# The mask of the soft-max: a GpSimd add one slot ahead in place of a bf16 matmul

## The chip, the core and the metric

The kernel runs on one core of a Trainium2 chip. The metric is device time in microseconds (us) of one execution. Five engines work side by side, each through its own queue in order: TensorE (PE: matmuls and transposes into PSUM), VectorE (DVE), ScalarE (ACT), GpSimd (POOL), and SyncE (SP), which issues the DMAs.

## The reference

Two layers over 512 positions of width 1024. Each projects `x`, runs two groups of eight attention heads, gates them, projects back and normalises. Group A is stick-breaking attention. Group B, to which the change belongs, is soft-max attention over the keys that an indexer picks:

```python
score = jnp.where(admissible[None], score, -jnp.inf)
vals, idx = lax.top_k(score, topk)
...
logits = jnp.einsum('bqhd,bqkhd->bqhk', qb, kg).astype(jnp.float32) * scale
bias = rel_bias[t5_bucket(idx - t[None, :, None])]
logits = logits + jnp.swapaxes(bias, -1, -2).astype(jnp.float32)
logits = jnp.where(valid[:, :, None, :], logits, -jnp.inf)
p = jax.nn.softmax(logits, axis=-1)
```

The kernel gathers nothing: it computes all logits of a block of 128 queries against the keys up to that block and adds a mask that is 0 for picked keys and -1e30 for the others.

## The kernel before, in words

Work is cut into blocks: one head, 128 queries (`qb` 0 to 3), with n = 128, 256, 384 or 512 keys. A layer has 24 blocks of the indexer, 32 of group A (`Stick`), 32 of group B (`Soft`); each starts in a slot of its own, slots 0 to 87 of the loop over `s`. The Soft blocks are slots 56 to 87: eight heads of four blocks, so `qb` is the slot's number modulo 4. The order of instructions on PE, ACT, DVE and POOL is the order of the code.

A Soft block passes through four slots:

- slot s: `stage0` puts the logits `z` into PSUM (a matmul at L399, the mask's at L401, a matmul at L402; the operands are split into a high and a low part). `z` has two PSUM buffers. `stage1` (DVE, L599) adds the position bias `gbias`, negates, writes `p` and keeps the row's minimum; `stage1b` (ACT, L604) takes the exponential and its row sums.
- slot s+1: `stage2`. In the last pair of heads (slots 80 to 87) it scales `p` by the reciprocal of the sums (L613 on DVE, L614 on ACT). In the other heads the reciprocals go through DRAM (`spread`), come back as the tile `over`, and POOL multiplies the pair's output by it later (L550).
- slot s+2: PE transposes `p` (L407), ACT copies the result to `AT` (L415), and DVE writes what that copy rounded off (L418).
- slot s+3, where the head's fourth block is that far: PE multiplies by the values (`o`, L556), ACT and DVE bring the two halves of `o` together (`mixt`, L464 and L466), and POOL multiplies them into `M` (L467). That is in slots 58, 62, ..., 86 for the head before.

Around these steps a slot is filled with projection matmuls (`pj`, `pjv`, `pjo`), by a table of due slots. Their weights come by DMA (`raw`), ACT rounds them to `whi` (L175), and POOL forms `wlo`, two instructions of 512 columns (L177). In slots 76, 79, 81 and 85 (`SPLITS`) ACT and POOL also split `M` for the output projection: `XH` on ACT (L144), then `XL` on POOL (L145).

On DVE, slot s has L599 of block s ahead of L418 of block s-2, and both ahead of `mixt`. On ACT, the exponential of block s stands ahead of the `XH` of that slot and of the copy of `mixt`.

## Time and profile before

| | |
|---|---|
| median of 3 runs | 674.58 us (674.5 to 675.34) |
| profiled execution, its own time | 674.73 us |
| its span, first to last instruction | 672.9 us |
| busy: PE, DVE, ACT, POOL | 659.6, 482.7, 351.5, 330.6 us |
| granted TensorE clock, mean | 0.997 |

The span is what the trace shows; the execution's time is 1.8 us longer. Busy shares are means over the whole span; what an engine's time is worth is read stage by stage. In the trace the Soft slots run from 208 to 298 us in the first layer and from 538 to 628 us in the second.

### The profile page before, as it was taken

The numbers are of one execution on the slowest core, as the hardware profiler recorded it, in microseconds if no ns is written. First come the engines' busy times: TensorE is split into PE (matmuls) and PEld (weight loads), VectorE is DVE, ScalarE is ACT, GpSimd is POOL, SyncE is SP. The second block draws the span as 40 slices with busy tenths as digits, with TensorE's granted clock in tenths as the row PEclk, the third lists the DMA queues.
The fourth block names the chain that finished last, engine by engine and source line by source line (L and its number), as shares of the span: only waits on it lengthen the run. The fifth ranks groups of instructions, "written<-read, shape, count | busy, mean of one in ns | idle before, by whom it ended". The sixth has DMA issues, their size and how long they took to land.

```text
span 672.9 us, 10299 instructions
## 1 busy us (share of the span) xinstructions
PE 659.6 (98%) x3575; PEld 553.7 (82%) x3589; DVE 482.7 (72%) x1019; ACT 351.5 (52%) x707; POOL 330.6 (49%) x303
## 2 busy tenths in 40 slices
PE   8999999999999999999999999999999999999995
PEld 4778988988889879877897888889888898897784
DVE  3588899999855455666853689999989554556576
ACT  4576545445447556773233765544534565568610
POOL 5343634466564433764354344445566533457531
PEclk9999999999999999999999999999999999999998
DMA  7625224242342354212125143432114534442022
GB/s 247 221 82 146 95 94 126 64 128 92 99 140 82 115 142 152 82 52 94 41 82 171 64 120 101 126 94 94 64 63 142 126 111 123 123 148 68 32 94 94
DMA packets 26203, 72.85 MB, mean 108 GB/s; under 512 B 5124, under 2 KB 6788, under 8 KB 26152
## 3 DMA queue, kind: packets, MB, share of 16 engines
q1 hardware_dynamic: 26152, 72.20, 34.4%
q8 instruction: 28, 0.46, 0.3%
q14 instruction: 23, 0.19, 0.1%
HBM read 58.87 MB, written 2.31 MB: 91 GB/s over the span
## 4 chain that ended last, share of the span: by engine, by line
PE 88%; DVE 5%; POOL 2%; DMA 2%; issue 1%; ACT 1%; SPq 1%; DVEq 0%; POOLq 0%; ACTq 0%
PE pj L221 14%; PE pj L222 14%; PE pj L223 14%; PE o L556 6%; PE tr L407 5%; PE z L402 4%; PE pjo L642 4%; PE pjo L644 4%; PE pjo L641 4%; PE z L399 4%; PE pjv L249 4%; PE pjv L248 4%; PE pjv L247 4%; POOL wlo L177 1%; DMA XN<-in_xt_dram 1%
## 5 line engine op out<-in xcount | busy, mean ns | idle before, releaser
L177 POOL TENSOR_TENSOR wlo<-raw,whi 128x512 fp32r<-128x512 f32 (+1 forms) x168 | 228.0, 1378 | 157.7 <-ACT whi L175 139.7
L221 PE MATMUL pj<-XH,whi 128*128 128x512 f32 (+1 forms) x456 | 185.4, 407 | 0.4 <-ACT whi L144 0.4
L222 PE MATMUL pj<-XL,whi 128*128 128x512 f32 (+1 forms) x456 | 178.9, 392 | 0.8 <-DVE XL L145 0.8
L223 PE MATMUL pj<-XH,wlo 128*128 128x512 f32 (+1 forms) x456 | 179.2, 393 | 0.0
L223 PEld LDWEIGHTS pj<-XH,wlo 128*128 128x128 f32 (+1 forms) x456 | 84.9, 186 | 20.3 <-POOL wlo L145 0.4
L175 ACT ACTIVATE whi<-raw 128x1024 fp32r<-128x1024 f32 (+1 forms) x87 | 91.2, 1050 | 19.9 <-PE pjo L642 6.6
L222 PEld LDWEIGHTS pj<-XL,whi 128*128 128x128 f32 (+1 forms) x456 | 85.4, 187 | 15.3 <-DVE XL L145 2.4
L221 PEld LDWEIGHTS pj<-XH,whi 128*128 128x128 f32 (+1 forms) x456 | 85.3, 187 | 15.1 <-ACT whi L144 1.1
L247 PE MATMUL pjv<-whi,XH 128*128 128x256 f32 x256 | 75.3, 294 | 0.0
L569 ACT ACTIVATE om<-z 128x128 f32<-128x128 f32 (+1 forms) x64 | 27.9, 437 | 86.9 <-PE z L402 80.7
L575 DVE TENSOR_TENSOR_SCAN om<-om 128x128 f32<-128x128 f32 (+1 forms) x64 | 69.3, 1082 | 5.1 <-POOL om L571 4.9
L249 PE MATMUL pjv<-wlo,XH 128*128 128x256 f32 x256 | 72.5, 283 | 0.3 <-POOL wlo L177 0.3
L248 PE MATMUL pjv<-whi,XL 128*128 128x256 f32 x256 | 72.2, 282 | 0.0
L467 POOL TENSOR_TENSOR M<-M,mixt 64x512 f32<-64x512 f32 x22 | 32.0, 1452 | 72.7 <-DVE mixt L466 39.3
L688 DVE MAX8 m<-scores 128x8 f32<-128x256 f32 (+2 forms) x96 | 52.8, 550 | 0.2
L689 DVE MATCH_REPLACE8 scores<-m,scores 128x256 f32<-128x256 f32 (+2 forms) x96 | 52.1, 542 | 0.0
L641 PE MATMUL pjo<-whi,XH 128*128 128x512 f32 x128 | 51.7, 404 | 0.0
L642 PE MATMUL pjo<-whi,XL 128*128 128x512 f32 x128 | 50.1, 391 | 1.6 <-DVE XL L145 1.6
L418 DVE TENSOR_TENSOR AT<-tr,AT 128x128 fp32r<-128x128 f32 (+1 forms) x64 | 31.3, 490 | 27.9 <-ACT AT L415 27.6
L644 PE MATMUL pjo<-wlo,XH 128*128 128x512 f32 x128 | 50.0, 391 | 0.0
L402 PE MATMUL z<-k,q 128*128 128x256 f32 (+2 forms) x128 | 49.3, 385 | 0.0
L249 PEld LDWEIGHTS pjv<-wlo,XH 128*128 128x128 f32 x256 | 48.6, 190 | 0.7 <-POOL wlo L177 0.7
(125 smaller groups left out, 1192.3 us busy)
## 6 DMA issues: line engine op xcount, KB each, us to landing
raw<-in_w_in_dram SPq DMA_DIRECT2D x70, 512.0 KB, 3.3
k<-k SPq DMA_DIRECT2D x32, 256.0 KB, 5.2
raw<-in_w_out_dram SPq DMA_DIRECT2D x16, 512.0 KB, 3.4
gbias<-f_dram SPq DMA_DIRECT2D x16, 256.0 KB
XN<-in_x_dram SPq DMA_DIRECT2D x4, 512.0 KB
out_dram<-XN SPq DMA_DIRECT2D x8, 256.0 KB, 2.1
M<-M SPq DMA_DIRECT2D x4, 448.0 KB
XN<-in_xt_dram SPq DMA_DIRECT2D x3, 512.0 KB
```

The source lines that it names most:

```text
L175: A.activation(hi[:, :n], raw[:, :n], AF.Copy)
L177: lo_engine.tensor_tensor(lo[:, c], raw[:, c], hi[:, c], ALU.subtract)
L221: T.matmul(o, w[0], XH[:, :, kc, :], start=first, stop=False)
L222: T.matmul(o, w[0], XL[:, :, kc, :], start=False, stop=False)
L223: T.matmul(o, w[1], XH[:, :, kc, :], start=False, stop=last)
L247: T.matmul(acc, XH[:, tb, kc, :], whi, start=kc == 0, stop=False)
L248: T.matmul(acc, XL[:, tb, kc, :], whi, start=False, stop=False)
L249: T.matmul(acc, XH[:, tb, kc, :], wlo, start=False, stop=kc == KC - 1)
L402: T.matmul(self.z[:, :nn], c, d, start=False, stop=True)
L641: T.matmul(acc, XH[:, tb, m, :], whi, start=n == 0, stop=False)
L642: T.matmul(acc, XL[:, tb, m, :], whi, start=False, stop=False)
L644: T.matmul(acc, XH[:, tb, m, :], wlo, start=False, stop=n == 2 * len(mts))
```

## The change

The mask's matmul and its bf16 identity `identb` go. A new step `prepare` allocates `p` and has POOL write into it the position bias (read backwards, as before) plus the mask (bf16). It runs one slot ahead: in slot s for block s+1, right after `stage0` of block s. DVE's `stage1` then adds `z` to `p` in place. The head's bias is loaded in `prepare` as well. The pool of `p` gets four buffers in place of three, and `over` one in place of two. In the changed file the numbers of lines are 2 to 4 lower in the middle of the program (L177 is L175, L467 is L463, L550 is L546, L145 is L143); the new add is L591, and DVE's step is L599 in both.

```diff
-    wk = ctx.enter_context(tc.tile_pool(name="wk", bufs=3))
+    wk = ctx.enter_context(tc.tile_pool(name="wk", bufs=4))
...
-        V.tensor_copy(identb, ident)
...
-            if mask is not None:
-                T.matmul(self.z[:, cols], identb, mask, start=False, stop=False, skip_group_check=True)
...
-                    st["over"] = tp.tile([P, S], F32, tag="over", name="over")
+                    st["over"] = tp.tile([P, S], F32, tag="over", name="over", bufs=1)
...
-            def stage0(self):
+
+            def prepare(self):
                 if self.qb == 0:
                     self.head.load()
-                self.product(*self.head.operands(), mask=mask[self.qb], cols=slice(0, self.n))
+                self.p = wk.tile([P, S], F32, tag="w", name="p")
+                G.tensor_tensor(self.p[:, : self.n], self.head.g[:, : self.n][:, ::-1], mask[self.qb], ALU.add)
+
+            def stage0(self):
+                self.product(*self.head.operands())
 
             def stage1(self):
                 h, n, b = self.head, self.n, slice(self.qb, self.qb + 1)
-                self.p = wk.tile([P, S], F32, tag="w", name="p")
                 p = self.p[:, :n]
-                V.tensor_tensor_reduce(out=p, in0=self.z[:, :n], in1=h.g[:, :n][:, ::-1], scale=-SCALE, scalar=3.0e38, op0=ALU.add, op1=ALU.min, accum_out=h.mn[:, b])
+                V.tensor_tensor_reduce(out=p, in0=self.z[:, :n], in1=p, scale=-SCALE, scalar=3.0e38, op0=ALU.add, op1=ALU.min, accum_out=h.mn[:, b])
...
             if at(s):
                 tasks[s].stage0()
+            if isinstance(at(s + 1), Soft):
+                tasks[s + 1].prepare()
             if at(s - 1) and s != IDX_SLOTS:
                 tasks[s - 1].stage2()
```

On POOL, from slot 74 of the first layer to slot 82, these rows stand in the kernel before (`wlo`: the low part of weights; `over`: the soft-max's reciprocals; `XL`: the low part of `M`):

```order
L467 TENSOR_TENSOR M<-M,mixt 64x512
L177 TENSOR_TENSOR wlo_2973<-raw_2759,whi_2972 128x512 x2
L550 TENSOR_TENSOR M<-M,over 128x512
L145 TENSOR_TENSOR XL<-M,XH 128x768
L467 TENSOR_TENSOR M<-M,mixt 64x512
L177 TENSOR_TENSOR wlo_3102<-raw_2899,whi_3101 128x512 x2
L145 TENSOR_TENSOR XL<-M,XH 128x768 x2
L467 TENSOR_TENSOR M<-M,mixt 64x512
```

In the changed kernel the same stretch of POOL's queue, down to the first of the two `XL` that share a row above, reads so (`p<-gbias,mask` is the new add):

```order
L463 TENSOR_TENSOR M<-M,mixt 64x512
L175 TENSOR_TENSOR wlo_2973<-raw_2759,whi_2972 128x512 x2
L591 TENSOR_TENSOR p<-gbias,mask_109 128x128
L546 TENSOR_TENSOR M<-M,over 128x512
L591 TENSOR_TENSOR p<-gbias,mask_110 128x256
L143 TENSOR_TENSOR XL<-M,XH 128x768
L591 TENSOR_TENSOR p<-gbias,mask_111 128x384
L591 TENSOR_TENSOR p<-gbias,mask_112 128x512
L463 TENSOR_TENSOR M<-M,mixt 64x512
L175 TENSOR_TENSOR wlo_3102<-raw_2899,whi_3101 128x512 x2
L591 TENSOR_TENSOR p<-gbias,mask_109 128x128
L143 TENSOR_TENSOR XL<-M,XH 128x768
```

The adds of blocks 76 to 80 now stand among rows that kept their order: the add of a head's first block is behind the product with `mixt` of slot 74 or 78 and the pair of `wlo` that follows it, and the adds of blocks 78 and 79 are ahead of the product with `mixt` of slot 78.

On DVE, slots 77 and 78 of the changed kernel, with what each instruction waits for (`ISA p,mn<-z,p` is L599; `AT` at L414 is the remainder of the transposed block, L418 before):

```order
L599 ISA p,mn<-z,p 128x256 [waits PE_49,Pool_49]
L599 ISA mn 128x1
L414 TENSOR_TENSOR AT_108<-tr,AT_107 128x4x128 [waits Activation_49]
L599 ISA p,mn<-z,p 128x384 [waits PE_49,Pool_49]
L599 ISA mn 128x1
L289 TENSOR_TENSOR vt<-pjv,vt 128x2x64 [waits Activation_49]
L289 TENSOR_TENSOR vt<-pjv,vt 128x2x64
L414 TENSOR_TENSOR AT_106<-tr,AT_105 128x128 [waits Activation_49]
L462 TENSOR_TENSOR mixt<-o,mixt 64x512 [waits Activation_49]
```

No row has moved on DVE, but L599 waits for POOL beside PE; before it waited for PE alone (`ISA p,mn<-z,gbias 128x256 [waits PE_49]`), and in a head's first block for the bias's DMA.

## Rows read from the trace of the kernel before

**Rows 1.** The page, parts 1 and 4: busy us and share by engine; the chain.

```profile
PE 659.6 (98%) x3575; PEld 553.7 (82%) x3589; DVE 482.7 (72%) x1019; ACT 351.5 (52%) x707; POOL 330.6 (49%) x303
PE 88%; DVE 5%; POOL 2%; DMA 2%; issue 1%; ACT 1%; SPq 1%; DVEq 0%; POOLq 0%; ACTq 0%
```

**Rows 2.** Timeline of PE, two Soft blocks: start us, us, line, op.

```profile
210.54 0.28 PE L399 MATMUL z<-k,q 128*128 128x256 f32 x1
210.66 0.28 PE L401 MATMUL z<-mask,identb 128*128 128x256 bf16 x1
210.70 0.37 PE L402 MATMUL z<-k,q 128*128 128x256 f32 x1
210.91 0.27 PE L247 MATMUL pjv<-whi,XH 128*128 128x256 f32 x1
...
245.01 0.39 PE L399 MATMUL z<-k,q 128*128 128x512 f32 x1
245.28 0.58 PE L402 MATMUL z<-k,q 128*128 128x512 f32 x1
245.69 0.39 PE L221 MATMUL pj<-XH,whi 128*128 128x512 f32 x1
```

**Rows 3.** Timeline of PE, two Stick blocks, which have no mask.

```profile
409.63 0.28 PE L399 MATMUL z<-k,q 128*128 128x256 f32 x1
...
409.87 0.40 PE L221 MATMUL pj<-XH,whi 128*128 128x512 f32 x1
...
419.01 0.39 PE L399 MATMUL z<-k,q 128*128 128x512 f32 x1
...
419.46 0.39 PE L221 MATMUL pj<-XH,whi 128*128 128x512 f32 x1
```

**Rows 4.** POOL's groups by form, 207.9 to 297.9 us: busy us, mean ns.

```profile
L177 POOL TENSOR_TENSOR wlo<-raw,whi 128x512 fp32r<-128x512 f32 x18 | 22.8, 1290 | 17.3 <-ACT whi L175 15.3 <-DMA gbias<-f_dram 1.7
L467 POOL TENSOR_TENSOR M<-M,mixt 64x512 f32<-64x512 f32 x8 | 10.3, 1289 | 24.5 <-issue 8.6 <-DVE mixt L466 7.9 <-PE z L402 7.4
L145 POOL TENSOR_TENSOR XL<-M,XH 128x768 fp32r<-128x768 f32 x4 | 7.3, 1840 | 3.4 <-ACT XH L144 3.4
L550 POOL TENSOR_TENSOR M<-M,over 128x512 f32<-128x512 f32 x3 | 3.9, 1291 | 1.0 <-DMA over<-r_dram 1.0
```

**Rows 5.** POOL's groups by form in the whole span: a smaller one.

```profile
L145 POOL TENSOR_TENSOR wlo<-raws,whi 128x256 fp32r<-128x256 f32 x6 | 6.1, 1032 | 0.0
```

**Rows 6.** POOL's busy us in two stretches of the first layer's Soft slots.

```profile
205.00:260.00 55.00, 23.08 (x20) 1.00 0.36 109
260.00:298.00 38.00, 23.78 (x17) 1.00 0.31 96
```

**Rows 7.** Timeline of POOL, slots 72 to 74.

```profile
264.20 2.54 POOL L177 TENSOR_TENSOR wlo<-raw,whi 128x512 fp32r<-128x512 f32 x2 [2.91 <-ACT whi L175]
270.13 1.29 POOL L467 TENSOR_TENSOR M<-M,mixt 64x512 f32<-64x512 f32 x1 [3.40 <-DVE mixt L466]
```

**Rows 8.** Timeline of DVE, slots 74, 77, 78, 85 and 87.

```profile
266.49 0.56 DVE L599 CUSTOM_DVE_ANT_0 p<-z,gbias 128x384 f32<-128x384 f32 x1 [0.63 <-PE z L402]
...
276.68 0.69 DVE L418 TENSOR_TENSOR AT<-tr,AT 128x512 fp32r<-128x512 f32 x1 [2.11 <-ACT AT L415]
277.29 0.55 DVE L599 CUSTOM_DVE_ANT_0 p<-z,gbias 128x384 f32<-128x384 f32 x1
...
279.50 0.68 DVE L466 TENSOR_TENSOR mixt<-o,mixt 64x512 f32<-64x512 f32 x1 [1.06 <-ACT mixt L464]
...
291.98 0.41 DVE L599 CUSTOM_DVE_ANT_0 p<-z,gbias 128x256 f32<-128x256 f32 x1
...
296.69 0.66 DVE L599 CUSTOM_DVE_ANT_0 p<-z,gbias 128x512 f32<-128x512 f32 x1
```

**Rows 9.** Timeline of ACT, slot 85 to the last product with the values.

```profile
293.37 0.83 ACT L144 ACTIVATE XH<-M 128x768 fp32r<-128x768 f32 x1
...
297.79 0.71 ACT L604 ACTIVATE p<-p,mn 128x512 f32<-128x512 f32 x1
...
303.22 0.59 ACT L464 ACTIVATE mixt<-o 64x512 f32<-64x512 f32 x1 [2.15 <-PE o L556]
```

**Rows 10.** The chain in order of time: the same step in either layer.

```profile
268.67 0.60 ACT mixt L464
...
598.33 0.60 ACT mixt L464
```

## The prediction

> **What bounds the kernel now.** I read the page first: PE is busy for 98% of the span and makes up 88% of the chain that ended last, while POOL is busy for 49% [rows 1]. So whatever is taken off PE should come off the time, unless another engine becomes late. A mean over the span does not tell whether POOL can take more, so I read it in the two parts of the Soft slots where its new work lands: 23.1 us of 55 in the first four heads (slots 56 to 71), but 23.8 of 38 in the last four (slots 72 to 87), where weights, the products into M and the XL splits all meet [rows 6]. Then I read POOL, DVE and ACT one instruction at a time through that second part, because there a slot is only a little over 2 us long.

> **What is removed: the mask matmuls.** PE's price is read from starts, since the ends of matmuls are modelled and overlap. With the mask, a block of 256 keys takes 0.37 us from the first matmul of z to the next work (210.54 to 210.91), a block of 512 takes 0.68 (245.01 to 245.69) [rows 2]. Blocks without a mask take 0.24 and 0.45 [rows 3]. The mask costs 0.13 and 0.23. A block of 128 keys runs the same 256 columns of z: 0.13. For 384 I take the middle, 0.18. A head saves 0.13 + 0.13 + 0.18 + 0.23 = 0.67 us, eight heads 5.35 per layer, two layers 10.7 us. That is the most the change can give. The cast of the identity in the prologue and the other operand of L599 (one f32 tile for another) I cost at nothing: the cast has all the prologue's DMA waits around it, and DVE still reads one operand of z and one from SBUF.

> **What is added: 64 adds on POOL.** The trace has no f32 plus bf16 add, so I bound it by POOL's other two-input instructions in the same slots: 1.29 us for 512 columns (wlo, and the products with over and, on 64 partitions, mixt), 1.84 for 768 [rows 4]. The difference gives 2.15 ns a column and 0.19 us fixed: 0.47, 0.74, 1.02 and 1.29 us for the four blocks, 3.52 us a head. As upper bound I take the 256-column instruction of the prologue, 1.03 us [rows 5], 1.39 times the 0.74; as lower bound 0.8 of the price, if a 2-byte operand should read faster. I take 1.0, since the rows of these very slots hardly scatter.

> [...]

> **Where the adds stand, and who waits.** The load alone is telling: in slots 73 to 87 POOL gets 13.6 us more, so it would be busy for 37.4 us in a stretch of 38 that is to shrink by 2.7. POOL works in order, and it also waits in that stretch. An add that is late holds L599; behind L599 on DVE stand the remainder of block s-2, which the product with the values needs, and mixt, for which POOL's next product waits. In the first four heads POOL is more than half idle and slots are longer; a late add there costs DVE a wait and PE nothing. Their saving, 4 x 0.67 = 2.7 us, I let stand. From slot 72 I follow POOL by hand, on the new clock (2.7 us earlier at slot 72).

> - wlo starts when ACT has rounded the weights: 264.20 before, now 261.5, to 264.1 [rows 7]. Behind it is the 384-add of block 74, to 265.1. L599 of block 74 started at 266.49 [rows 8], without the wait it would start at 263.6; it starts at 265.15.
> - From the start of such an L599 to the end of mixt is 2.9 us (277.29 to 279.50 + 0.68 in slot 78 [rows 8]): L599, the exponential, the copy of o, mixt. So POOL's product into M of slot 74 starts at 268.05; it was 270.13 [rows 7].
> - From there to the end of the last add (block 87) POOL's queue holds, by the order shown: three products with mixt (3.87), two pairs of wlo (5.16), two with over (2.58), four XL (7.36), three heads of adds (10.56): 29.5 us.
> - Three waits come on top. In slot 78 POOL does the 384-add, then the 512-add (1.29), then needs mixt, which follows 2.9 us after the 384-add: 1.6 us idle. In slots 81 and 85 the 256-add is followed by the 384-add (1.02) and then by XL, which needs XH, and ACT does XH only after that block's exponential: from the start of L599 to the end of XH is 2.2 us (291.98 to 293.37 + 0.83 [rows 8, 9]), so 1.2 us idle, less what ACT gains by being free, 1.1 each. With 0.1 at the first XL that is 3.9 us.
> - The last add therefore ends at 268.05 + 29.5 + 3.9 = 301.45. L599 of block 87 started at 296.69 before [rows 8], and would start at about 291.4 if PE alone set the pace. Now it starts at 301.5.
> - From that L599 to the copy of the last o took 6.5 us (303.22 - 296.69); ACT was then busy with another block for 0.4 us after L599's end (296.69 + 0.66 to 297.79) [rows 8, 9], which falls away: 6.1. The copy is at 307.6 in place of 303.22, 4.35 us later.

> So PE's 5.35 us are lost whole and 4.3 us more, in each layer; the second layer repeats the first (the same step of the chain at 268.67 and at 598.33 [rows 10]). PE's remaining projection work and the tail of a layer follow in order and shift by the same. The stall begins in slot 77: DVE's remainder of block 75 started at 276.68 [rows 8]; PE is 3.1 us ahead by then, yet behind the 256-add of block 77 it comes only about 1.5 us earlier.

> **Sum.** 674.73 (the profiled execution's own time, 0.15 above the median) + 2 x 4.3 = 683.3; against the median, **683.2 us**. The pools I cost at nothing: p has four buffers for four slots of life, the bias of a head is loaded when the head three before it has been read, and the one buffer of over is read by POOL about two slots before the next pair writes it.

> **The rivals.**

> - *The saving arrives whole*: 674.6 - 10.7 = 663.9. For it stands the 98% of PE. Against it: block 87's add would have to end at about 291.4, ten us earlier, on a path of 33.4 whose adds are 10.56. That needs a PE that doesn't feel a late L599; but z has two buffers, so PE feels one that is two slots late, and in slots of some 2 us the lateness reaches that.
> - *Half of it*: the late heads break even with PE's pace of before, the early heads keep 2.7 us per layer: 674.6 - 5.4 = 669.2. It ends on the other side by one mechanism: POOL's path from slot 74 to the last add falls to 33.4 - 7.0 = 26.4 us; below 33.4 - 4.3 = 29.1 the change begins to win. The three waits would have to vanish and the adds cost 0.7 of my price.
> - *No change*: the path is at 29.1, 674.6. If the adds are as priced and POOL never waits, it is at 29.5.
> - *Dearer adds*: at the prologue's 1.39 the path grows by 4.1 us a layer: 691.4. It holds if f32 plus bf16, or reading backwards, is slower on POOL than what the trace has there.

> **How the numbers follow.** Two executions agree within about 0.1%, so 0.2% (1.3 us) is about what can be told from no change. Chances: the forecast 0.62 (its own range, adds at 0.8 to 1.2 of the price, 2.1 us a layer each way: 679 to 688), dearer adds 0.08, no change 0.10, half 0.14, whole 0.06. Slower is 0.70, the same 0.10, faster 0.20. A range that leaves out the whole saving, and the far parts of half and of dearer adds, is 669 to 691.

> **What the profile after would show.** Right: no L401; 64 groups of p<-gbias,mask on POOL near 0.47, 0.74, 1.02 and 1.29 us; Soft slots up to 71 shorter by 0.13 to 0.23 us each; from slot 74 POOL at 85% or more with idle time put down to mixt and XH; DVE's L599 waiting for POOL in slots 76 to 87 by 2 us and more; PE idle before transposes and o in the late Soft slots, some 4.3 + 5.35 = 9.7 us a layer. The last product with the values of the first layer starts about 4 us later than before. Wrong: adds far from 1.29 us at 512 columns, or L599 waiting for PE as before while POOL idles.

## The result, and the profile after

The changed kernel takes 682.15 us (median of 4 runs, 680.71 to 682.99), the kernel before 674.73 (4 runs, 674.5 to 675.34). The ratio is 1.0106, 95% interval 1.0085 to 1.0128: about 7.4 us slower. The profiled execution took 682.9 us, with a span of 681.1.

The first and fourth part of the page after: busy time by engine, and the chain that ended last by engine.

```profile
PE 657.9 (97%) x3525; PEld 555.5 (82%) x3525; DVE 483.4 (71%) x1018; ACT 352.8 (52%) x707; POOL 380.2 (56%) x367
PE 76%; POOL 8%; DVE 6%; ACT 4%; issue 3%; DMA 2%; SPq 1%; DVEq 0%; POOLq 0%; ACTq 0%
```

Beside [rows 1] POOL has 64 instructions and 49.6 us more. PE has lost little busy time, but its share of the chain fell by 12 points: POOL has 6 more, ACT 3, DVE 1, and 2 are issue. How dear the adds are, in POOL's groups by form (busy us, mean ns):

```profile
L591 POOL TENSOR_TENSOR p<-gbias,mask 128x512 f32<-128x512 f32 x16 | 18.9, 1179 | 0.0
L591 POOL TENSOR_TENSOR p<-gbias,mask 128x384 f32<-128x384 f32 x16 | 15.3, 954 | 0.4 <-PE tr L403 0.4
L591 POOL TENSOR_TENSOR p<-gbias,mask 128x256 f32<-128x256 f32 x16 | 10.8, 678 | 0.0
L591 POOL TENSOR_TENSOR p<-gbias,mask 128x128 f32<-128x128 f32 x16 | 6.9, 428 | 0.2
```

A head's four adds sum to 3.24 us. Where the time goes is read from PE, at the first matmul of z in slot 72 (the fifth head's first block, 128 keys in 256 columns) and in slot 87 (the eighth head's last block, 512). Timeline of PE before, then after:

```profile
261.41 0.28 PE L399 MATMUL z<-k,q 128*128 128x256 f32 x1
...
295.61 0.39 PE L399 MATMUL z<-k,q 128*128 128x512 f32 x1
```

```profile
259.68 0.28 PE L397 MATMUL z<-k,q 128*128 128x256 f32 x1
...
299.52 0.39 PE L397 MATMUL z<-k,q 128*128 128x512 f32 x1
```

From slot 72 to slot 87 it was 34.20 us and is 39.84. From slot 54, just ahead of the Soft slots, to slot 72 it was 63.70 (197.71 to 261.41) and is 61.14 (198.54 to 259.68). So the early heads gain 2.56 us and the late ones lose 5.64. In the second layer the same rows give a gain of 1.96 (63.03 to 61.07) and a loss of 5.86 (34.22 to 40.08). The four together are a loss of 6.98 of the 7.4 us; the rest lies outside the Soft slots. (Slot 54 comes at another time from profile to profile, before the change can act: -1.21 to +0.92 us against the kernel before. So what follows compares these two stretches and not the absolute starts.)

How POOL went through the late slots, in its timeline (in brackets: idle us before the instruction, and what ended it):

```profile
268.64 1.29 POOL L463 TENSOR_TENSOR M<-M,mixt 64x512 f32<-64x512 f32 x1 [1.75 <-DVE mixt L462]
270.01 2.54 POOL L175 TENSOR_TENSOR wlo<-raw,whi 128x512 fp32r<-128x512 f32 x2
272.51 0.43 POOL L591 TENSOR_TENSOR p<-gbias,mask 128x128 f32<-128x128 f32 x1
272.89 1.29 POOL L546 TENSOR_TENSOR M<-M,over 128x512 f32<-128x512 f32 x1
274.13 0.68 POOL L591 TENSOR_TENSOR p<-gbias,mask 128x256 f32<-128x256 f32 x1
275.13 1.82 POOL L143 TENSOR_TENSOR XL<-M,XH 128x768 fp32r<-128x768 f32 x1 [0.32 <-ACT XH L142]
276.92 2.04 POOL L591 TENSOR_TENSOR p<-gbias,mask 128x384 f32<-128x384 f32 x2
280.92 1.27 POOL L463 TENSOR_TENSOR M<-M,mixt 64x512 f32<-64x512 f32 x1 [1.97 <-DVE mixt L462]
...
289.42 1.85 POOL L143 TENSOR_TENSOR XL<-M,XH 128x768 fp32r<-128x768 f32 x1 [1.04 <-ACT XH L142]
...
298.19 1.86 POOL L143 TENSOR_TENSOR XL<-M,XH 128x768 fp32r<-128x768 f32 x1 [1.16 <-ACT XH L142]
300.00 1.19 POOL L591 TENSOR_TENSOR p<-gbias,mask 128x512 f32<-128x512 f32 x1
```

And DVE, in the same stretch:

```profile
272.97 0.29 DVE L599 CUSTOM_DVE_ANT_0 p<-z,p 128x128 f32<-128x128 f32 x1 [2.38 <-POOL p L591]
...
275.57 0.69 DVE L414 TENSOR_TENSOR AT<-tr,AT 128x512 fp32r<-128x512 f32 x1 [0.30 <-ACT AT L411]
277.87 0.56 DVE L599 CUSTOM_DVE_ANT_0 p<-z,p 128x384 f32<-128x384 f32 x1 [1.60 <-POOL p L591]
...
278.35 0.48 DVE L289 TENSOR_TENSOR vt<-pjv,vt 128x128 fp32r<-128x128 f32 x2
...
301.22 0.69 DVE L599 CUSTOM_DVE_ANT_0 p<-z,p 128x512 f32<-128x512 f32 x1 [0.53 <-POOL p L591]
```

Where an L599 waits for POOL, it begins as its add ends (272.51 + 0.43 and 272.97; 300.00 + 1.19 and 301.22). POOL in turn waits for mixt, which DVE makes behind such an L599 and ACT behind its exponential, and for XH. Before, L599 had not waited for POOL at all; now the waits of the whole span hold this line (us, times, longest):

```profile
DVE p L599 <- POOL p L591: 30.0, 24, 2.4
```

So 24 of the 64 L599 wait for their add. From there it goes to PE, whose timeline reads so in slot 78 and at the start of slot 79:

```profile
275.60 0.50 PE L552 MATMUL o<-AT,vt 128*128 128x512 f32 x1 [1.02 <-ACT AT L411]
...
278.70 0.80 PE L552 MATMUL o<-AT,vt 128*128 128x256 f32 x2 [0.54 <-DVE vt L289]
279.29 0.63 PE L397 MATMUL z<-k,q 128*128 128x512 f32 x1
```

The product with the values (`o`) waits for the transposed block, and then for `vt`, which DVE writes at 278.35, right behind the L599 of 277.87 that had waited 1.60 us for its add. In the kernel before, PE's one wait in the same stretch (257 to 303 us) was 0.23 us.

Four windows (us; busy time and instructions of PE, PEld, DVE, ACT, POOL; granted clock; DMA):

```profile
257.00:303.00 46.00, 42.19 (x249) 36.24 (x248) 24.56 (x82) 31.91 (x80) 36.49 (x34) 0.93 0.24 77
...
272.00:277.00 5.00, 3.42 (x18) 2.35 (x17) 2.29 (x8) 2.82 (x9) 4.68 (x6) 0.94 0.35 108
277.00:282.00 5.00, 4.46 (x15) 3.58 (x14) 2.88 (x9) 3.10 (x6) 3.03 (x3) 0.50 0.07 26
282.00:287.00 5.00, 5.00 (x27) 4.14 (x25) 1.33 (x6) 2.85 (x8) 5.00 (x6) 0.88 0.23 62
```

PE stands still for 3.8 us of the 46, 1.6 of them from 272 to 277; in the 5 us behind that its granted clock is 0.50. The 0.94 and 0.88 on either side hold a little more of it: in shorter windows the clock is 1.00 from 270.0 to 276.0, 0.88 to 276.5, 0.50 in each from there to 283.0, 0.79 to 283.5, and 1.00 again from there to 287.0. That is an estimated 6.8 us at 0.50, if the two mixed windows hold 1.00 and 0.50 alone. The 512-column matmul of z at 279.29 took 0.63 us where it takes 0.39 at 299.52, at a clock of 1.00. Whether the clock or the waiting sets the time can't be read from this page.

### The profile page after: what moved, and what is told of

The parts are those of the page before. It is cut to its first block, busy times and chain, and to the rows that moved or that the text cites. A ratio compares the mean times of both kernels' runs of the same rounds, so it can differ in the third digit from the quotient of the medians.

```text
span 681.1 us, 10344 instructions
## 1 busy us (share of the span) xinstructions
PE 657.9 (97%) x3525; PEld 555.5 (82%) x3525; DVE 483.4 (71%) x1018; ACT 352.8 (52%) x707; POOL 380.2 (56%) x367
## 4 chain that ended last, share of the span: by engine, by line
PE 76%; POOL 8%; DVE 6%; ACT 4%; issue 3%; DMA 2%; SPq 1%; DVEq 0%; POOLq 0%; ACTq 0%
PE pj L219 14%; PE pj L220 14%; PE pj L221 14%; PE o L552 4%; PE tr L403 4%; PE pjv L247 3%; PE pjv L245 3%; PE pjv L246 3%; PE z L397 3%; PE z L398 3%; PE pjo L642 3%; PE pjo L644 3%; PE pjo L641 3%; POOL wlo L175 3%; POOL p L591 2%
## 5 line engine op out<-in xcount | busy, mean ns | idle before, releaser
L175 POOL TENSOR_TENSOR wlo<-raw,whi 128x512 fp32r<-128x512 f32 (+1 forms) x168 | 228.5, 1382 | 141.5 <-ACT whi L173 133.8
L571 DVE TENSOR_TENSOR_SCAN om<-om 128x128 f32<-128x128 f32 (+1 forms) x64 | 71.1, 1111 | 5.8 <-POOL om L567 5.6
L599 DVE CUSTOM_DVE_ANT_0 p<-z,p 128x128 f32<-128x128 f32 (+1 forms) x64 | 31.2, 488 | 45.2 <-POOL p L591 30.0
L463 POOL TENSOR_TENSOR M<-M,mixt 64x512 f32<-64x512 f32 x22 | 31.9, 1452 | 49.4 <-DVE mixt L462 38.3
L552 PE MATMUL o<-AT,vt 128*128 128x256 f32 (+2 forms) x256 | 50.6, 336 | 6.1 <-DVE AT L414 2.3
L552 PEld LDWEIGHTS o<-AT,vt 128*128 128x128 f32 x256 | 42.7, 193 | 13.8 <-DVE AT L414 4.5
L567 POOL TENSOR_SCALAR_AFFINE_SELECT om<-om 128x128 f32<-128x128 f32 x64 | 23.0, 360 | 52.3 <-ACT om L565 46.3
```

Source lines behind the costliest of these rows:

```text
L175: lo_engine.tensor_tensor(lo[:, c], raw[:, c], hi[:, c], ALU.subtract)
L552: T.matmul(self.o[:, q0 * P :], vt[:, sb, self.hh * P : (self.hh + 1) * P], at_block(self.at[j], sb, q0, NTB - q0), start=n == 0, stop=n == 7)
L571: V.tensor_tensor_scan(rev, rev, rev, 1.0, ALU.mult, ALU.min)
```

## The experiments

The theory: POOL's late adds hold L599, and the late L599 holds PE in the last four heads. Rivals: POOL's load alone counts, wherever in its queue an add stands; the adds cost by running at all beside the others; PE's clock; the pools. All ratios are to the kernel before, run on the same chip (675.03, 675.46 and 675.17 us in the three series; only the changed kernel itself is set against 674.73).

**Only the early, only the late heads.** The mask goes to POOL in half of the heads; the others keep the matmul.

```diff
                 self.head = head
+                self.on_pool = head.pair < 6
...
+                if not self.on_pool:
+                    return
                 G.tensor_tensor(self.p[:, : self.n], self.head.g[:, : self.n][:, ::-1], mask[self.qb], ALU.add)
```

The late one has `head.pair >= 6`.

> The adds on POOL only in the first four soft-max heads (slots 56 to 71); the last four heads keep the mask's matmul; pools as in the changed kernel. If POOL's queue in the late slots is the cause, the early saving stays whole: 674.7 - 2 x 2.7 = 669.3, L599 waits for POOL at most a few times and briefly, PE's clock stays at its upper level. If one buffer of over, or a fourth of p, costs the time, or adds on POOL cost wherever they stand, it is at or above 674.7.

> The reverse: the adds only in the last four heads (slots 72 to 87), the mask's matmul in the first four. If POOL's path from slot 74 to the last add sets the pace, it starts 2.7 us later in each layer and is as long as in the changed kernel: 682.2 + 5.4 = 687.5, slower than the changed kernel. If the loss came from PE running ahead of POOL by what the early heads saved, the late heads alone would lose less: 678 to 682.

Measured: early 671.34 us, 0.9943 [0.9929, 0.9958]; late 687.87, 1.0188 [1.0171, 1.0205]. Both parts of the prediction's sum are there on their own. By stretches: with the early heads alone slots 54 to 72 take 61.15 and slots 72 to 87 take 34.21, unchanged; with the late ones alone 63.70, unchanged, and 39.86. The late loss is the same whether PE comes early or not. The late kernel came out as expected; the early one is 2.0 us above the 669.3. Its two stretches give 4.5 us (2.56 and 1.95) in place of 5.4, and the rest of the miss lies outside them.

**No mask at all** (the add is taken out, L599 reads the bias; the mask is left out of the computation):

```diff
-                G.tensor_tensor(self.p[:, : self.n], self.head.g[:, : self.n][:, ::-1], mask[self.qb], ALU.add)
...
-                V.tensor_tensor_reduce(..., in1=p, ...)
+                V.tensor_tensor_reduce(..., in1=h.g[:, :n][:, ::-1], ...)
```

> The mask is left out altogether, neither matmul nor add (every key up to the block's end is attended). It measures what PE gives back when nobody waits for POOL. By the starts of the matmuls 674.7 - 10.7 = 664.0. If ACT or DVE bound the late slots anyway (ACT is busy for 30.1 of 38 us there), only the early heads' 5.4 and a part of the rest: 666 to 669.

Measured: 669.12 us, 0.9913 [0.9898, 0.9927]. So 5.9 us, and not 10.7, is all that taking the mask off PE can give. The early stretch gives its 2.56; the late one takes 33.77 in place of 34.20, so 0.43 where the matmuls of its fifteen blocks were priced at 2.45 (four heads at 0.67, less the last block's 0.23). The window of the late slots of this kernel, columns as above:

```profile
260.00:298.00 38.00, 36.27 (x227) 31.43 (x227) 21.91 (x75) 30.58 (x77) 25.16 (x19) 1.00 0.26 84
```

PE now idles 1.7 us (0.3 in the same window before), and its waits in the stretch are for ACT's AT and p and DVE's AT; ACT is busy for 30.58 of 38 us.

**The adds without anyone waiting.** The kernel before, with 64 such adds into a tile that nobody reads:

```diff
+                spare = tp.tile([P, S], F32, tag="spare", name="spare", bufs=1)
+                G.tensor_tensor(spare[:, : self.n], self.head.g[:, : self.n][:, ::-1], mask[self.qb], ALU.add)
...
+                self.product(*self.head.operands(), mask=mask[self.qb], cols=slice(0, self.n))
```

> The kernel before with the 64 adds on POOL besides, at the places where the changed kernel has them, but into a tile that nobody reads; the mask's matmul stays, and L599 waits for PE alone. If the late add that L599 waits for is the cause, POOL's load alone costs little: 675 to 678. If the load is the cause by making the products into M, XL and wlo late, it costs like the changed kernel: 682 or more, since the mask's matmuls are still there.

Measured: 676.38 us, 1.0018 [1.0009, 1.0028]. Slots 72 to 87 take 34.59 us against 34.20. All of POOL's added work costs 1.4 us when no L599 depends on it.

**The pools alone** (kernel before, four buffers for p, one for over: `wk` 4, `over` `bufs=1`).

> The kernel before with the pools of the changed one alone: four buffers for p, one for over; the mask's matmul stays. If the pools cost nothing, 674.7 within 0.2%. If one buffer of over makes SP wait and holds the weights' loads behind it, slower by some us.

Measured: 675.43 us, 1.0001 [0.9991, 1.0011]. Nothing.

**PE kept busy through its stall.** Eight matmuls of 512 columns ahead of the values in slot 78; their result is overwritten.

```diff
                 self.o = po.tile([P, S], F32, tag="o", name="o")
+                if self.pair == 6 and self.s == 0:
+                    q, slot, k, ks = self.operands()
+                    for _ in range(8):
+                        T.matmul(self.o, q[:, slot, 0:P], k[:, ks, :], start=True, stop=True)
```

> The changed kernel with eight extra matmuls of 512 columns (1.8 us at the upper clock) in slot 78 of each layer, written into o just before the product with the values that PE waits for there; their results are overwritten. They keep PE active in the idle time after which its clock fell to half for 6.8 us in each layer. If POOL's path sets the pace and the clock is only a consequence, no more than the slower product with the values is won back, 0.7 us a layer: about 680.8, or the same. If the halved clock is what costs, some 3 us a layer: 676.

Measured: 682.8 us, 1.0115 [1.0098, 1.0132]. In the profiled execution (681.79 us) the mean granted clock is 0.996 against 0.986; in the other three it is 0.988 to 0.990 (682.72 to 683.83 us), so it is the profiled one that tells. The window of the second layer's late slots, after and then with the eight matmuls:

```profile
605.00:630.00 25.00, 20.39 (x99) 16.38 (x98) 12.15 (x42) 15.44 (x39) 21.51 (x22) 0.86 0.17 54
```

```profile
605.00:630.00 25.00, 20.22 (x106) 15.88 (x104) 12.96 (x44) 16.45 (x43) 21.41 (x21) 1.00 0.16 55
```

With a granted clock of 1.00 over the window, slots 72 to 87 of that layer take 39.84 us (592.29 to 632.13) against 40.08. In the first layer the clock fell later (0.66 from 287.5 to 292.5 us, 1.00 before that from 260 on), and was 0.96 on average over the same slots in place of 0.91: 39.97 us against 39.84. The lower clock stretched matmuls that would have waited anyway; it is not the cause.

**Less for POOL, in the same order.** From slot 74 on, the products with mixt run on DVE.

```diff
-                mix(done.head.pair, done.head.s, done.head.o, V if last else G)
+                mix(done.head.pair, done.head.s, done.head.o, V if last or s >= 74 else G)
```

> The changed kernel with the products of M and mixt from slot 74 on done by DVE (0.69 us each there) in place of POOL. POOL's path from slot 74 to the last add, 32.6 us in the changed kernel's trace, loses three products (3.9) and the wait for mixt in slot 78 (2.0): the last add ends about 5.8 us earlier, at 295.3; that is 1.4 us later than the kernel without a mask would need it, so 682.2 - 2 x 5 = 672. If DVE's own waits for POOL are what counts and not the path's length, it stays near 680.

Measured: 682.45 us, 1.0101 [1.0086, 1.0116]. The expectation failed by 10 us. POOL lost four products a layer, three of them (3.9 us) on the path to the last add, but that add ended at 300.11 in place of 301.19, and not at the 295.3 expected. Slots 72 to 87 became shorter by 0.8 and 1.1 us (39.07 and 38.99), and what lies behind them longer by 0.9 and 0.8; why is open. POOL's timeline:

```profile
268.64 2.70 POOL L175 TENSOR_TENSOR wlo<-raw,whi 128x512 fp32r<-128x512 f32 x2 [2.04 <-ACT whi L173]
...
279.97 2.79 POOL L175 TENSOR_TENSOR wlo<-raw,whi 128x512 fp32r<-128x512 f32 x2 [2.20 <-ACT whi L173]
...
297.12 1.85 POOL L143 TENSOR_TENSOR XL<-M,XH 128x768 fp32r<-128x768 f32 x1 [3.06 <-ACT XH L142]
```

The waits for mixt became waits for whi, which ACT rounds in order behind the exponential and the copy of o, and a longer one for XH. It isn't a clean subtraction: two of the products took 1.06 and 1.07 us on DVE beside POOL's adds, and two pairs of `wlo` 2.70 and 2.79 in place of 2.54. Even so the path is not the sum of POOL's work, as the expectation had it, but a loop through three queues. The other reading was put to the test in the same series, by the next run: what counts is how early an add stands in POOL's queue.

**The adds one place earlier.** Prepared two slots ahead in place of one, behind the `evacuate` of the slot; four buffers are still enough.

```diff
-            if isinstance(at(s + 1), Soft):
-                tasks[s + 1].prepare()
...
                 old.evacuate(old.head.at)
+            if isinstance(at(s + 2), Soft):
+                tasks[s + 2].prepare()
```

> The changed kernel with each add placed one slot earlier still: in slot s for block s+2, behind the transposes of slot s, ahead of that slot's XL and product with mixt; four buffers still do. POOL's work is the same, only its place in the queue differs. If order is what makes the adds late (each stands behind a product, weights and XL that wait for blocks before it), most of the loss goes: 671 to 674. If POOL simply has too much to do in the late slots, little changes: 679 to 682.

Measured: 674.38 us, 0.9984 [0.9975, 0.9993], just above the 671 to 674 expected from order. With the same work on POOL, the late stretch takes 36.21 us in place of 39.84 (in the second layer 37.03 in place of 40.08). The waits of L599 and two rows of POOL's timeline:

```profile
DVE p L599 <- POOL p L591: 8.5, 6, 1.6
```

```profile
276.04 1.58 POOL L591 TENSOR_TENSOR p<-gbias,mask 128x512 f32<-128x512 f32 x2
278.20 1.29 POOL L463 TENSOR_TENSOR M<-M,mixt 64x512 f32<-64x512 f32 x1 [0.58 <-DVE mixt L462]
```

POOL's wait for mixt in slot 78 falls from 1.97 to 0.58 us, and the 30.0 us of DVE's waits to 8.5. What holds the late slots above the 33.77 without a mask is not settled; from 257 to 303 us L599 still waits 4.2 us for adds (11.4 in the changed kernel).

**Order without load.** The order of the changed kernel, each add cut to 8 columns. L599 still waits for it but takes the bias alone, so the mask is left out here too.

```diff
-                G.tensor_tensor(self.p[:, : self.n], self.head.g[:, : self.n][:, ::-1], mask[self.qb], ALU.add)
+                G.tensor_tensor(self.p[:, 0:8], self.head.g[:, 0:8], mask[self.qb][:, 0:8], ALU.add)
```

> The changed kernel with each add cut to 8 columns, at the same place in POOL's queue; L599 still waits for it, but takes the bias alone, so the mask is left out. POOL's added load is nearly gone, its order is not. If load is the cause, it is as fast as the kernel without any mask: 669. If order and waits are the cause as well (a small add too stands behind weights, products and XL that wait for ACT), the last add ends only some 4.7 us earlier than in the changed kernel and 673 to 674 remains.

Measured: 675.93 us, 1.0017 [1.0007, 1.0027], above both expectations, and nearer to that of the order. The group of the adds, and POOL's waits in its timeline:

```profile
L591 POOL TENSOR_TENSOR p<-gbias,mask 128x8 f32<-128x8 f32 x64 | 12.4, 205 | 4.1 <-PE tr L403 3.9
```

```profile
277.39 1.28 POOL L463 TENSOR_TENSOR M<-M,mixt 64x512 f32<-64x512 f32 x1 [2.66 <-DVE mixt L462]
...
285.16 1.84 POOL L143 TENSOR_TENSOR XL<-M,XH 128x768 fp32r<-128x768 f32 x1 [1.75 <-ACT XH L142]
...
294.32 1.85 POOL L143 TENSOR_TENSOR XL<-M,XH 128x768 fp32r<-128x768 f32 x1 [3.02 <-ACT XH L142]
```

Four adds of a head cost 0.8 us in place of 3.24, and the late stretch still takes 37.60 us against 33.77 with none. POOL waits longer for mixt and XH than in the changed kernel. So 6.8 of the 13.0 us between no mask (669.1) and the change (682.2) remain where the adds keep their place and lose nearly all their work; 6.2 go with the work. Taken the other way, with the work kept and the adds one slot earlier, 7.8 go (682.15 to 674.38) and 5.3 remain: by either measure each of the two is roughly half of the loss.

**Both** (two slots ahead, and the products on DVE).

> Adds two slots ahead, and the late products with mixt on DVE besides. If what remains in the kernel with adds two slots ahead (674.4 against 669.1 without a mask) is POOL's load, taking away four products of 1.29 us a layer gives 671 to 672. If DVE and ACT wait for each other by then, the products on DVE cost as much as they free: 674 to 675.

Measured: 673.67 us, 0.9986 [0.9977, 0.9995], which its interval does not tell from two slots ahead alone (0.9984). Slots 72 to 87 are shorter by 0.9 and 1.7 us, and what lies behind them is again longer, by 0.5 and 0.6. Load taken off POOL helps little in either order.

**A version that beats both.** Two slots ahead, and only the first five heads on POOL; the last three keep the matmul.

```diff
+                self.on_pool = head.pair < 6 or (head.pair, head.s) == (6, 0)
```

> Adds two slots ahead on POOL in the first five heads of a layer (slots 56 to 75), the mask's matmul in the last three. Each head with an add saves PE 0.67 us as long as no late block depends on POOL: five heads, two layers, 6.7 us at most; the prologue of the changed kernels took up to 0.9 more. 668.5 to 670, faster than the kernel before by 0.8%, and than the first four heads alone (671.3). If the adds for slots 72 to 75 already meet the late POOL work, it is no faster than 671.

Measured: 668.07 us, 0.9908 [0.9894, 0.9922], a little better than the 668.5 to 670 expected. The two stretches take 61.14 and 33.77 us, exactly those of no mask at all, and so they do in the second layer (60.44 and 33.77): in the last three heads the mask matmul costs nothing. DVE's step is L609 in this file; its waits hold no entry for POOL any more, and the one for PE's matmuls is

```profile
DVE p L609 <- PE z L402: 15.5, 22, 1.2
```

The first layer's stretches and the times side by side (us; the kernel before took between 674.73 and 675.46 in the series that these times come from):

| kernel | slots 54 to 72 | slots 72 to 87 | time |
|---|---|---|---|
| before | 63.70 | 34.20 | 674.73 |
| after | 61.14 | 39.84 | 682.15 |
| early heads only | 61.15 | 34.21 | 671.34 |
| late heads only | 63.70 | 39.86 | 687.87 |
| no mask | 61.14 | 33.77 | 669.12 |
| two slots ahead | 61.14 | 36.21 | 674.38 |
| adds of 8 columns | 61.14 | 37.60 | 675.93 |
| two ahead, five heads | 61.14 | 33.77 | 668.07 |

## Why the prediction was right, point by point

The direction and the mechanism were right, and the 683.2 us are 1.05 above the 682.15 measured. That it is so near is in part luck: terms that were off in opposite directions. The late loss was 7.0 us a layer and came as 5.64 and 5.86, 2.5 us too much in all; the early gain was 2.7 a layer and came as 2.56 and 1.96, 0.9 too much. So 8.6 us were forecast where the stretches show 7.0, and another 0.4 lies outside them. Two things, the clock and DVE's scan, were not in the prediction.

- *The price of the adds.* 0.47, 0.74, 1.02 and 1.29 us were forecast; 0.428, 0.678, 0.954 and 1.179 came, 3.24 a head for 3.52. The difference over columns is 1.96 ns a column (1179 - 428 over 384), with 0.18 us fixed. The lower bound of 0.8 of the price was the author's estimate and stood on no row; the adds came at 0.92 of it.
- *The price of the matmuls.* In the first layer, slots 56 to 71 became shorter by 0.09 to 0.24 us each, a head by 0.64 for the 0.67 forecast. "A block of 128 keys runs the same 256 columns" is true of z and not of the mask's matmul, which has 128 columns there; those blocks gained 0.10 to 0.12 for 0.13.
- *POOL's path from slot 74.* The product into M was to start at 268.05 and started at 268.64. The waits of 1.6, 1.1 and 1.1 us came as 1.97, 1.04 and 1.16, at the three places named, and the 0.1 at the first XL as 0.32. The last add was to end at 301.45 and ended at 301.19, L599 of block 87 to start at 301.5 and started at 301.22: a cheaper price, longer waits. The copy of the last o was to come at 307.6, and came at 307.38 (303.22 in [rows 9]), 4.16 us later; forecast were 4.35. These starts agree better than they should: slot 54 came 0.83 us later in this profile than in the one before, which the change didn't do. Measured from z of slot 72, the last add ended 41.5 us later where the working has 42.7, and the path from slot 74 took 32.55 us for 33.4.
- *The early heads.* 2.7 us a layer were let stand; 2.56 and 1.96 came, and the run with the early heads alone is 3.7 us faster in all. That a late add costs PE nothing there was right in the first layer only (below).
- *The late heads.* The sum had PE lose its gain of 2.7 us and 4.3 more, 7.0 from slot 72 on. It lost 5.64 and 5.86. "The last product with the values of the first layer starts about 4 us later" came as 4.16 at the copy behind that product, and as 3.91 at z of slot 87; 0.83 of either is the later slot 54.
- *The most the change can give.* 10.7 us was wrong by almost half. The working took the price of a matmul on PE as time on the path; without the mask, PE waits for ACT and DVE in the late slots, and the rest is 5.9 us. The rival of the whole saving, 663.9, therefore could not have come, whatever POOL did, and the rival of half of it, 669.2, is what leaving the mask out altogether gives. This step didn't enter the sum, since the late saving was taken to be lost, but it gave that rival its 0.06.
- *PE idle "some 4.3 + 5.35 = 9.7 us a layer"*: 3.8 us stand idle in the window shown. The lower clock, which wasn't foreseen, fills more of it: at 0.50 z's first matmul of 512 columns starts 0.43 us ahead of its second (279.29, 279.72) and at 1.00 it starts 0.23 ahead (299.52, 299.75); from 280 to 282 us, at 0.50, all 2.00 us pass for busy. The run with eight added matmuls shows that this hid the wait and didn't make it.
- *POOL at 85% or more from slot 74*: from 268.6 to 301.2 it is busy 27.82 of 32.60 us, 85%.
- *L599 waiting for POOL "in slots 76 to 87 by 2 us and more"* came in slots 76 and 80 alone (2.38 and 2.29). The others wait 0 to 1.6 us; block 87's waits 0.53 and yet starts 4.53 us later than before, so the wait of one L599 does not show how late it is.
- *The view of POOL as one queue with a length*, on which "half of it" and "no change" rested ("below 29.1 the change begins to win"), is what the experiments took down. Taking 3.9 us of products off the path (to DVE) brought its end forward by 1.1 us and gave nothing in all, and adds of 8 columns still left a loss in the late slots. In the changed kernel an add stands behind POOL's products and splits of its slot, these behind mixt, whi and XH, and these behind the L599 that waits for the add before. Where one member is shortened, the next wait grows. That opening this loop helps is shown by the adds one place earlier (674.38) and by leaving the last four heads out of it (34.21 us from slot 72 to 87). Adds three slots ahead weren't tried.

The layers differ by one thing that was not foreseen. Of the second layer's early gain 0.6 us are lost at one place, between slots 57 and 58, where the scan of block 55 on DVE runs longer. Before, POOL was idle beside it; after, it has an add. DVE's scan before:

```profile
538.10 1.22 DVE L575 TENSOR_TENSOR_SCAN om<-om 128x512 f32<-128x512 f32 x1
```

DVE's scan and POOL's add after:

```profile
542.59 2.58 DVE L571 TENSOR_TENSOR_SCAN om<-om 128x512 f32<-128x512 f32 x1 [0.40 <-POOL om L567]
```

```profile
542.53 1.56 POOL L591 TENSOR_TENSOR p<-gbias,mask 128x256 f32<-128x256 f32 x2
```

It is 0.6 us of the early gain in this layer (1.96 beside 2.56), and the only place where PE feels it: in the changed kernel PE waits 0.44 us for om there, with the early heads alone 0.45. That the adds are the cause is shown by the runs at hand. Slots 54 to 72 of the second layer take 61.07 us in the changed kernel, but 60.44 without a mask and with adds of 8 columns, where that scan takes 1.23 and 1.22 us, and 60.44 with adds two slots ahead, where it takes 1.69.

## What to carry to other kernels

What work costs on an engine that is half idle can depend on its place in that engine's queue as much as on its duration: look for the loop that goes from the moved instruction through the engines that wait for it and back to its own queue, and issue it early enough to open that loop, or keep it out of the stretch. A saving on the busiest engine is worth only what the next engine leaves of it, stage by stage; a kernel with the work left out altogether gives that ceiling in one run, here 5.9 us for matmuls priced at 10.7. Moving only the part that lies in the slack stretch can beat both all and nothing: five heads of eight gave the whole ceiling.
